# A hybrid encoder step: sums of squares on GpSimd, a root moved into the head, and three reorderings

## The chip, the cores and the metric

The kernel runs on one core of a Trainium2 chip. A core has a matrix engine (TensorE, PE in the profile, with weight loads as PEld), a vector engine (VectorE, DVE), a scalar engine (ScalarE, ACT), GpSimd (POOL) and SyncE (SP), which here only issues DMAs. Each engine works through its own queue in order; semaphores order the engines among each other. SBUF is the memory on the core, PSUM the accumulators that TensorE writes. The metric is the device time of one execution in microseconds (us), lower is better.

## The reference

One layer of a streaming encoder, for 512 new frames of a prompt and 32 of a running stream, D = 2048:

```
xn = rmsnorm(x, g_mix)
z = xn @ w_in                    # conv gates, h, q, k, v and 8 forget logits
x = x + concat(rmsnorm(gated short conv), rmsnorm(forgetting attention)) @ w_out
x = x + cross_attention(rmsnorm(x, g_xattn), 256 memory tokens) @ w_xo
x = x + square(relu(rmsnorm(x, g_mlp) @ w_up)) @ w_down      # hidden 8192
y = rmsnorm(x, g_final)
```

`rmsnorm` divides by the root of the mean square over the 2048 channels of a frame. Beside y, the new keys, values, forget values, conv rows and memory keys and values are returned. All is float32.

## The kernel before

Activations lie with channels on the 128 partitions and the T = 544 frames along the row, so x is 16 tiles of 128x544, read in two column halves of 272. Each float32 operand is split (`split`, L84 and L85) into a high part, rounded by ScalarE to the matrix engine's format, and a low part, the rest, subtracted by VectorE; each product is three matmuls (high-high, high-low, low-high). Most of the large products are done in a seven-product form (Strassen's kind): sums and differences of weight blocks ("sum", L230 and L1261) and of activation blocks ("operands", L199 to L213, whose sums are `ts`) are formed on VectorE.

A norm's sum of squares is kept per frame in two 128x544 accumulators, one for each half of the 16 tiles: ScalarE squares a tile into a buffer `sq`, and a DMA issued by GpSimd adds it to the accumulator in SBUF. `rstd` (L170 on) then sums over partitions by TensorE (`ssq`), and takes the root by ScalarE's Ln and Exp and four VectorE instructions per half. Since g is applied to the rows first, the root r is multiplied in after the product.

The stages, by time: the **head** (0 to 60 us), eight steps j, each with two tiles of x (`xr`), 512 KB of weights, the operands, and 48 matmuls into eight PSUM halves (L362 to L394), which are then copied to the `first_tiles` hr, gc, gb, hr; the forget logits (`emit_logf`, L430, to 70 us); the pairs of in-projection products, conv gating and attention (to 870); memory values and the cross-attention output, called **xo** here (917 to 960), which per tile m adds to the reloaded x (`x2r`), stores it (`x3d`), squares it and applies the gain; the MLP's up products (960 to 1655); the down products (1650 to 2333), whose 8 output pairs p are gone through in four chunks c, with forms of the hidden rows stored to DRAM (`fd`, `bd`) by GpSimd and loaded again; and the **end** (2333 to 2365), four last products of 2x2 kind (L1380 to L1401), the last root (`last_rstd`) and the stores of y.

The order of each engine's queue is set when the kernel is built. A scheduler puts out instructions in the order in which the code emits them, except that it fills idle time with later work that is ready, and that weight splits and roots carry a higher priority. So code that is moved may or may not move instructions. Buffers come from pools of a fixed depth: `tmp` has 7 slots for sq, x2r, h and others; `rstd` has 3, which the forms' `fp` use too; the MLP's `raw2` has 4.

The function `begin` runs between the products of the first pair: it takes the root of x, multiplies the four first tiles by it (L579), hands them to the gating code `kinds`, and evacuates the forget logits (`evac_logf`, z at L435). `forms_in_parts` (L1177 on) gives three steps for each of the last two hidden rows, `differences`, `first` (four `put`s) and `second` (four `put`s), one of which runs after each output pair p of the first chunk.

Of the kernel before, what the change touches and what calls it, by code (L numbers as in the profile page):

```python
# [8 lines left out]
F32 = mybir.dt.float32  # L9
F32R = mybir.dt.float32r  # L10
AF = mybir.ActivationFunctionType
ALU = mybir.AluOpType
# [11 lines left out]
H = 8  # L24
# [17 lines left out]
def hybrid_step(  # L42
# [115 lines left out]

    def accumulate(acc, sq, first):
        if first:  # L160
            dve.tensor_copy(acc, sq)
        else:
            dve.tensor_tensor(acc, acc, sq, ALU.add)
# [35 lines left out]
    def operands(x, b11, ts, tags):  # L199
        hi, lo = two(b11)[:, 0], two(b11)[:, 1]  # L200
        split(hi, lo, x[:, 0])
# [160 lines left out]
    for j in range(8):  # L362
        xr = [headp.tile([128, T], F32, tag="xr", name="xr", bufs=5) for i in range(2)]
        if j == 0:
            hi, lo = weights(w_first[j])
        for i in range(2):
            sp.dma_start(xr[i], xT[j + 8 * i])
        if j:
            hi, lo = weights(w_first[j])
        x = headp.tile([128, 4, TH], F32, tag="x", name="x", bufs=2)  # L370
        for i in range(2):
            if j + i == 0:
                dve.tensor_scalar(x[:, :2], two(xr[i]), gain(G_MIX, 0), None, ALU.mult)
# [14 lines left out]
        for i in range(2):  # L388
            if j:
                sq = tmp("sq")[:, :T]  # L390
                act.activation(sq, xr[i], AF.Square)
                pool.dma_start(acc_x[i], sq, accum_op=ALU.add)
            else:
                act.activation(acc_x[i], xr[i], AF.Square)  # L394
# [13 lines left out]
    for t, ps in ((2, heads[2]), (3, heads[3]), (0, heads[0]), (1, heads[1])):  # L408
        for a in range(2):
            act.activation(two(first_tiles[t])[:, a], ps[a], AF.Copy)  # L410
# [161 lines left out]
    ps = emit_logf()  # L572
    nxt = fetch_pair(0)
    box = {}

    def begin():
        rstd(acc_x, D, out=rb)
        for t, (n, j) in enumerate((("hr", 0), ("gc", 0), ("gb", 0), ("hr", 1))):
            dve.tensor_tensor(first_tiles[t], first_tiles[t], rb, ALU.mult)  # L579
# [513 lines left out]
    def xo_done(m, ps):  # L1093
# [4 lines left out]
        if j == 0:  # L1098
            act.activation(acc_3[i], x, AF.Square)
        else:  # L1100
# [390 lines left out]
```

## Time and profile before

| | us |
|---|---|
| median of 3 runs | 2367.64 (2362.61 to 2367.76) |
| the profiled execution's own time | 2366.75 |
| its span | 2364.9 |
| busy: TensorE, VectorE, ScalarE, GpSimd | 2310.9, 2008.1, 1317.8, 246.8 |
| mean granted TensorE clock | 0.994 |
| accumulating DMAs (acc<-sq) | 40 of 272 KB, 4.9 to landing |
| first product of the head | 8.24 after the span's start |
| last product | ended about 2351; the span ends at 2364.9 |

TensorE is the bound over nearly the whole span. In the page's 40 slices its busy share is below nine tenths only in the first slice, and in slices at the xo stage, the forms and the end. Idle time in brackets in the time lines is the time for which an engine stood before an instruction, and behind the arrow is what ended it.

### The profile page before, as it was taken

How to read it: one execution, taken by the hardware profiler on the slowest of the kernel's cores; microseconds unless marked ns; L12 is line 12 of the kernel's file. 1: busy time of each engine (PE TensorE's matmuls, PEld its weight loads, DVE VectorE, ACT ScalarE, POOL GpSimd, SP SyncE). 2: the span in 40 equal slices, each digit the busy share in tenths (PEclk: the TensorE clock that was granted, in tenths of full speed). 3: DMA queues.
4: the chain of work that ended last, by engine and by line, in shares of the span. 5: the costliest groups of instructions: out<-in, count | busy, mean ns of one | idle time of the engine just before them, and what ended most of it. 6: DMA issues, size and time to landing. Idle time of an engine off the chain costs nothing. (4 is left out here: it accounts for less than half of the span.)

```text
span 2364.9 us, 47573 instructions
## 1 busy us (share of the span) xinstructions
PE 2310.9 (98%) x18083; PEld 2281.7 (96%) x18083; DVE 2008.1 (85%) x3562; ACT 1317.8 (56%) x2569; POOL 246.8 (10%) x447
## 2 busy tenths in 40 slices
PE   8999999999999999899999999999899999999997
PEld 8899999999999998899999999999799999999997
DVE  7899988877767757999999999998788888888885
ACT  8454555555644546665566656665455555555564
POOL 2000011113200001111111111111000000000001
PEclk9999999999999999999999999999999999999998
DMA  9333345578434537655666556668773564565454
GB/s 249 117 105 129 109 159 167 164 233 306 145 93 153 161 104 221 204 192 190 203 191 203 182 188 202 192 196 290 272 252 129 206 240 159 171 234 208 128 174 123
DMA packets 169638, 434.31 MB, mean 184 GB/s; under 512 B 19960, under 2 KB 24752, under 8 KB 169408
## 3 DMA queue, kind: packets, MB, share of 16 engines
q1 hardware_dynamic: 111616, 315.90, 39.8%
q0 software_dynamic: 52288, 106.45, 15.4%
q10 hardware_dynamic: 5504, 8.93, 1.1%
q8 instruction: 141, 2.31, 0.4%
q14 instruction: 89, 0.73, 0.1%
HBM read 322.27 MB, written 97.78 MB: 178 GB/s over the span
## 5 line engine op out<-in xcount | busy, mean ns | idle before, releaser
L84 ACT ACTIVATE whi<-raw 128x512 fp32r<-128x512 f32 x661 | 416.5, 631 | 466.8 <-PE mmx L269 95.4
L84 ACT ACTIVATE whi<-sum 128x512 fp32r<-128x512 f32 x676 | 422.4, 630 | 416.5 <-PE mmx L269 186.2
L85 DVE TENSOR_TENSOR wlo<-raw,whi 128x512 fp32r<-128x512 f32 x661 | 453.4, 688 | 123.5 <-ACT whi L84 115.8
L85 DVE TENSOR_TENSOR wlo<-sum,whi 128x512 fp32r<-128x512 f32 x676 | 453.1, 686 | 88.1 <-ACT whi L84 85.3
L1276 PE MATMUL dx<-f,whi 128*128 128x272 f32 x2016 | 389.6, 289 | 14.3 <-ACT e L1350 7.9
L269 PE MATMUL mmx<-oph,wlo 128*128 128x272 f32 x1296 | 374.9, 289 | 2.6 <-DVE wlo L85 2.6
L269 PE MATMUL mmx<-oph,whi 128*128 128x272 f32 x1296 | 373.5, 288 | 1.3 <-ACT h L278 0.9
L269 PE MATMUL mmx<-opl,whi 128*128 128x272 f32 x1296 | 372.1, 287 | 0.0
L1276 PEld LDWEIGHTS dx<-f,whi 128*128 128x128 f32 x2016 | 317.6, 189 | 16.5 <-ACT e L1350 9.7
L1276 PE MATMUL mm<-f,whi 128*128 128x272 f32 x1512 | 292.1, 288 | 0.0
L1276 PE MATMUL dx<-f,wlo 128*128 128x272 f32 x1008 | 291.3, 289 | 0.0
L269 PE MATMUL mmy<-oph,whi 128*128 128x272 f32 x864 | 249.8, 289 | 6.3 <-ACT whi L84 5.1
L269 PE MATMUL mmy<-oph,wlo 128*128 128x272 f32 x864 | 249.1, 289 | 0.9 <-DVE wlo L85 0.9
L269 PE MATMUL mmy<-opl,whi 128*128 128x272 f32 x864 | 248.8, 288 | 0.0
L269 PEld LDWEIGHTS mmx<-oph,wlo 128*128 128x128 f32 x1296 | 244.0, 188 | 3.2 <-DVE wlo L85 3.2
L269 PEld LDWEIGHTS mmx<-oph,whi 128*128 128x128 f32 x1296 | 244.7, 189 | 1.9 <-ACT h L278 1.1
L269 PEld LDWEIGHTS mmx<-opl,whi 128*128 128x128 f32 x1296 | 244.2, 188 | 0.0
L1276 PEld LDWEIGHTS mm<-f,whi 128*128 128x128 f32 x1512 | 238.2, 189 | 0.0
L1276 PE MATMUL mm<-f,wlo 128*128 128x272 f32 x756 | 218.1, 289 | 0.0
L1276 PEld LDWEIGHTS dx<-f,wlo 128*128 128x128 f32 x1008 | 190.6, 189 | 0.0
L269 PEld LDWEIGHTS mmy<-oph,whi 128*128 128x128 f32 x864 | 162.9, 189 | 7.5 <-ACT whi L84 5.5
L269 PE MATMUL mmx<-b,whi 128*128 128x272 f32 x864 | 167.8, 291 | 1.3 <-DVE x2r L1095 1.1
(412 smaller groups left out, 4941.5 us busy)
## 6 DMA issues: line engine op xcount, KB each, us to landing
raw<-in_w_up SPq DMA_DIRECT2D x128, 512.0 KB, 3.8
raw<-in_w_dn SPq DMA_DIRECT2D x128, 512.0 KB, 4.6
f<-fd SPq DMA_DIRECT2D x224, 272.0 KB, 5.7
fd<-form POOLq DMA_DIRECT2D x180, 272.0 KB, 4.0
raw<-in_w_in SPq DMA_DIRECT2D x88, 512.0 KB, 3.9
raw<-in_w_out SPq DMA_DIRECT2D x32, 512.0 KB, 3.9
acc<-sq POOLq DMA_DIRECT2D x40, 272.0 KB, 4.9
kq<-hl POOLq DMA_DIRECT2D x32, 256.0 KB, 3.1
```

Of the source, the lines that this page charges most:

```text
L84: act.activation(hi, src, AF.Copy)
L85: dve.tensor_tensor(lo, src, hi.bitcast(F32), ALU.subtract)
L269: pe.matmul(ps, a[:, c], x, start=first and j == 0 and n == 0, stop=j == 7 and n == 2, skip_group_check=not first)
L1276: pe.matmul(ps, a[:, c], f[:, x], start=first and j == 0 and n == 0, stop=j == 3 and n == 2, skip_group_check=not first)
```

## The change

Six edits that leave what is computed as it is.

1. The new helper `pool_sum` replaces the accumulating DMA in xo (`acc_3`) and in the last chunk (`acc_4`): ScalarE squares into a `tmp` buffer and GpSimd adds. In the head GpSimd also takes the squares themselves.
2. In the head's first step the loads go xr, half of the weights, xr, the other half; VectorE's first tile and the splits of b12 and b11 stand ahead of the second tile.
3. The eight PSUM halves of the head are copied in the order 0, 2, 3, 1, the first column half by ScalarE and the second by VectorE.
4. The root of x, the four multiplications (now on GpSimd) and `evac_logf` are emitted right behind the forget logits. `begin` keeps the scaled root and the gating.
5. `forms_in_parts` gives nine steps per hidden row, one `put` each; one step is run after each output pair, past the first chunk if need be.
6. At the end, of the first half's outputs two are done by VectorE and three by GpSimd ahead of the last product's addition, the other three by VectorE behind it; a store of y is one piece of 2176 bytes per partition, in a new layout of the output array that the host undoes.

```
@@ -156,6 +156,12 @@
     def gain(off, k):
         return vec[:, off + k:off + k + 1]
 
+    def pool_sum(acc, src, first):
+        sq = acc if first else tmp("sq")[:, :T]
+        act.activation(sq, src, AF.Square)
+        if not first:
+            pool.tensor_tensor(acc, acc, sq, ALU.add)
+
     def accumulate(acc, sq, first):
         if first:
             dve.tensor_copy(acc, sq)
@@ -198,7 +204,6 @@
 
     def operands(x, b11, ts, tags):
         hi, lo = two(b11)[:, 0], two(b11)[:, 1]
-        split(hi, lo, x[:, 0])
         t = ts.rearrange("p (a b c) -> p a b c", a=2, b=2)
         x4 = x.rearrange("p (a b) c -> p a b c", a=2)
         o = {"b11": (hi, lo)}
@@ -361,21 +366,35 @@
     xops = []
     for j in range(8):
         xr = [headp.tile([128, T], F32, tag="xr", name="xr", bufs=5) for i in range(2)]
+        if j:
+            for i in range(2):
+                sp.dma_start(xr[i], xT[j + 8 * i])
+            hi, lo = weights(w_first[j])
+        else:
+            raws = [wpool.tile([128, 1024], F32, tag="raw", name="raw", bufs=3)[:, :512] for i in range(2)]
+            for i in range(2):
+                sp.dma_start(xr[i], xT[8 * i])
+                sp.dma_start(raws[i], w_first[0, :, 512 * i:512 * i + 512])
+            hi, lo = halves(raws[0], 512)
+        x = headp.tile([128, 4, TH], F32, tag="x", name="x", bufs=2)
         if j == 0:
-            hi, lo = weights(w_first[j])
+            dve.tensor_scalar(x[:, :2], two(xr[0]), gain(G_MIX, 0), None, ALU.mult)
+        else:
+            for i in range(2):
+                act.activation(x[:, 2 * i:2 * i + 2], two(xr[i]), AF.Identity, scale=gain(G_MIX, j + 8 * i))
         for i in range(2):
-            sp.dma_start(xr[i], xT[j + 8 * i])
-        if j:
-            hi, lo = weights(w_first[j])
-        x = headp.tile([128, 4, TH], F32, tag="x", name="x", bufs=2)
-        for i in range(2):
-            if j + i == 0:
-                dve.tensor_scalar(x[:, :2], two(xr[i]), gain(G_MIX, 0), None, ALU.mult)
-            else:
-                act.activation(x[:, 2 * i:2 * i + 2], two(xr[i]), AF.Identity, scale=gain(G_MIX, j + 8 * i))
+            sq = tmp("sq")[:, :T] if j else acc_x[i]
+            pool.tensor_tensor(sq, xr[i], xr[i], ALU.mult)
+            if j:
+                pool.tensor_tensor(acc_x[i], acc_x[i], sq, ALU.add)
         b12 = two(headp.tile([128, T], F32R, tag="b12", name="b12", bufs=2))
         split(b12[:, 0], b12[:, 1], x[:, 1])
         b11 = formp.tile([128, T], F32R, tag="b11", name="b11")
+        split(two(b11)[:, 0], two(b11)[:, 1], x[:, 0])
+        if j == 0:
+            act.activation(x[:, 2:], two(xr[1]), AF.Identity, scale=gain(G_MIX, 8))
+            more = halves(raws[1], 512)
+            hi, lo = Parts([hi, more[0]]), Parts([lo, more[1]])
         o = operands(x, b11, headp.tile([128, 2 * T], F32, tag="ts", name="ts"), "ABC")
         xops.append(o)
         for i, xs in enumerate(((o["b11"], (b12[:, 0], b12[:, 1])), (o["b21"], o["b22"]))):
@@ -385,13 +404,6 @@
                     for a in range(2):
                         pe.matmul(ps[a], w[:, c], xs[a][q], start=j + i == 0 and n == 0,
                                   stop=j + i == 8 and n == 2)
-        for i in range(2):
-            if j:
-                sq = tmp("sq")[:, :T]
-                act.activation(sq, xr[i], AF.Square)
-                pool.dma_start(acc_x[i], sq, accum_op=ALU.add)
-            else:
-                act.activation(acc_x[i], xr[i], AF.Square)
     wf_hl = tpool.tile([128, T + 4], F32R, tag="t", name="wf_hl")[:, :256].rearrange("p (k c) -> p k c", k=KD)
     split(wf_hl[:, :, 0:8], wf_hl[:, :, 8:16], wf)
     head_cm.__exit__(None, None, None)
@@ -405,9 +417,9 @@
         return keepp.tile([128, T + 4], F32, tag="keep", name=name)
 
     first_tiles = [tmp("hr0")[:, :T], tmp("gc0")[:, :T], tmp("gb0")[:, :T], kept("hr1")[:, :T]]
-    for t, ps in ((2, heads[2]), (3, heads[3]), (0, heads[0]), (1, heads[1])):
-        for a in range(2):
-            act.activation(two(first_tiles[t])[:, a], ps[a], AF.Copy)
+    for t in (0, 2, 3, 1):
+        act.activation(two(first_tiles[t])[:, 0], heads[t][0], AF.Copy)
+        dve.tensor_copy(two(first_tiles[t])[:, 1], heads[t][1])
 
     rb = npool.tile([128, T], F32, tag="rstd", name="rb", bufs=3)
     rbs = npool.tile([128, T], F32, tag="rstd", name="rbs", bufs=3)
@@ -570,16 +582,16 @@
 
     steps = (lambda: gate_open(box["z"]), gate_exp, gate_log, gate_close, gate_sum, turn_logf)
     ps = emit_logf()
+    rstd(acc_x, D, out=rb)
+    for t in range(4):
+        pool.tensor_tensor(first_tiles[t], first_tiles[t], rb, ALU.mult)
+    box = {"z": evac_logf(ps)}
     nxt = fetch_pair(0)
-    box = {}
 
     def begin():
-        rstd(acc_x, D, out=rb)
+        dve.tensor_scalar(rbs, rb, SCALE, None, ALU.mult)
         for t, (n, j) in enumerate((("hr", 0), ("gc", 0), ("gb", 0), ("hr", 1))):
-            dve.tensor_tensor(first_tiles[t], first_tiles[t], rb, ALU.mult)
             kinds[n][1](j, first_tiles[t])
-        box["z"] = evac_logf(ps)
-        dve.tensor_scalar(rbs, rb, SCALE, None, ALU.mult)
 
     def job(i):
         (n1, j1), (n2, j2) = pairs[i]
@@ -1095,17 +1107,13 @@
         dve.tensor_tensor(two(x), two(x), ps[:, :, :TH], ALU.add)
         sp.dma_start(x3d[m], x)
         j, i = m % 8, m // 8
-        if j == 0:
-            act.activation(acc_3[i], x, AF.Square)
-        else:
-            sq = (tmp("sq") if j > 4 else up.tile([128, 1024], F32, tag="raw2", name="sq", bufs=4))[:, :T]
-            act.activation(sq, x, AF.Square)
-            pool.dma_start(acc_3[i], sq, accum_op=ALU.add)
+        pool_sum(acc_3[i], x, j == 0)
         if i == 0:
             xgs[j] = up.tile([128, 2 * T], F32, tag="sum", name="x").rearrange("p (a b) -> p a b", a=4)
         act.activation(xgs[j][:, 2 * i:2 * i + 2], two(x), AF.Identity, scale=gain(G_MLP, m))
         if i:
             b11 = upform.tile([128, T], F32R, tag="b11", name="b11")
+            split(two(b11)[:, 0], two(b11)[:, 1], xgs[j][:, 0])
             ops.append(operands(xgs.pop(j), b11, up.tile([128, 2 * T], F32, tag="sum", name="ts"), "ABC"))
 
     def fetch_up(i, last=True):
@@ -1191,18 +1199,13 @@
             dve.tensor_tensor(t12[:, 1], b[:, 1], t12[:, 0], ALU.subtract)
             dve.tensor_tensor(t34[:, 1], b[:, 0], t12[:, 1], ALU.subtract)
 
-        def first():
-            put(fd[i][0], a[:, 0])
-            put(bd[i - NF + 4], a[:, 1])
-            put(fd[i][5], b[:, 0])
-            put(fd[i][3], b[:, 1])
-
-        def second():
-            for t, q in zip(box["t"], ((1, 2), (4, 6))):
-                for n in range(2):
-                    put(fd[i][q[n]], t[:, n])
-
-        return [differences, first, second]
+        steps = [differences]
+        for dst, x in ((fd[i][0], a[:, 0]), (bd[i - NF + 4], a[:, 1]), (fd[i][5], b[:, 0]), (fd[i][3], b[:, 1])):
+            steps.append(lambda dst=dst, x=x: put(dst, x))
+        for n, q in enumerate(((1, 2), (4, 6))):
+            for k in range(2):
+                steps.append(lambda n=n, k=k, q=q: put(fd[i][q[k]], box["t"][n][:, k]))
+        return steps
 
     rb_3 = []
 
@@ -1309,20 +1312,14 @@
         return r
 
     def store(p, a, y):
-        d = slice(TH * a, TH * a + TH)
-        (sp if p % 2 else act).dma_start(o_y[2 * p:2 * p + 2, :, d].rearrange("m p t -> p m t"), two(y))
+        (sp if p % 2 else act).dma_start(o_y[a, p], y)
 
     def complete(p):
         for a in range(2):
             fin[a, p] = slot("AB"[a], F32, "yout")
         for i in range(2):
             m = 2 * p + i
-            if p == 0:
-                act.activation(acc_4[i], x3[m], AF.Square)
-            else:
-                sq = tmp("sq")[:, :T]
-                act.activation(sq, x3[m], AF.Square)
-                pool.dma_start(acc_4[i], sq, accum_op=ALU.add)
+            pool_sum(acc_4[i], x3[m], p == 0)
             for a in range(2):
                 act.activation(two(fin[a, p])[:, i], two(x3[m])[:, a], AF.Identity, scale=gain(G_FIN, m))
 
@@ -1366,8 +1363,8 @@
             dve.tensor_tensor(xb[:, 0], xb[:, 0], X, ALU.add)
             if c + 1 < NF // 4 and p < 7:
                 nf[p] = load_form(c + 1, p)
-            if c == 0 and 1 <= p <= len(parts):
-                parts[p - 1]()
+            if parts and c + p:
+                parts.pop(0)()
             if c == NF // 4 - 1:
                 complete(p)
         if c < NF // 4 - 1:
@@ -1377,6 +1374,12 @@
     ws = [[doperand(a11), doperand(a12)], [doperand(a21), doperand(a22)]]
     hs = ((fs[0], fs[5]), (b12, fs[3]))
     sums = []
+
+    def pooled(r):
+        rp = tmp("rb")[:, :TH]
+        act.activation(rp, r, AF.Copy)
+        return rp
+
     for a in range(2):
         y = fin[a, 7] = slot("AB"[a], F32, "yout")
         sums.append([t[:, TH * a:TH * a + TH] for t in acc_4])
@@ -1394,14 +1397,17 @@
             act.activation(sq, xa, AF.Square)
             sums[a].append(sq)
             act.activation(two(y)[:, i], xa, AF.Identity, scale=gain(G_FIN, 14 + i))
-            if a:
-                if i == 0:
-                    rb_4 = last_rstd(sums[0])
-                for p in range(4 * i, 4 * i + 4):
+            if a and i == 0:
+                rb_4 = last_rstd(sums[0])
+                rb_5 = pooled(rb_4)
+                for p in (0, 1):
                     store(p, 0, finish((0, p), rb_4, dve))
+                for p in (2, 3, 4):
+                    store(p, 0, finish((0, p), rb_5, pool))
+    for p in (5, 6, 7):
+        store(p, 0, finish((0, p), rb_4, dve))
     rb_4 = last_rstd(sums[1])
-    rb_5 = tmp("rb")[:, :TH]
-    act.activation(rb_5, rb_4, AF.Copy)
+    rb_5 = pooled(rb_4)
     for p in range(8):
         store(p, 1, finish((1, p), rb_5 if p in (2, 4, 7) else rb_4, pool if p in (2, 4, 7) else dve))
     down_cm.__exit__(None, None, None)
...
```

What the order of the instructions shows at three places. **GpSimd in the head**: before, the 14 accumulating DMAs stand in one block behind the constants:

```order
L146 MEMSET mask_p 128x128
L194 MEMSET sel_111 16x8
L147 AFFINE_SELECT mask_p<-mask_p 128x128
L196 AFFINE_SELECT sel_111<-sel_111 16x8 x2
L392 DMA acc<-sq 128x544 x14
L535 DMA yd_0_902<-ych 128x544
```

and after the change, from the second tile on and at the end of the block:

```order
L387 TENSOR_TENSOR acc<-xr 128x544
L202 AFFINE_SELECT sel_111<-sel_111 16x8
L387 TENSOR_TENSOR sq<-xr 128x544 x2
L389 TENSOR_TENSOR acc<-acc,sq 128x544 x2
L387 TENSOR_TENSOR sq<-xr 128x544
L389 TENSOR_TENSOR acc<-acc,sq 128x544
...
L389 TENSOR_TENSOR acc<-acc,sq 128x544
L587 TENSOR_TENSOR hr_887<-hr_887,rb 128x544
L587 TENSOR_TENSOR gc_888<-gc_888,rb 128x544
L587 TENSOR_TENSOR gb_889<-gb_889,rb 128x544
L587 TENSOR_TENSOR hr_890<-hr_890,rb 128x544
L547 DMA yd_0_904<-ych 128x544
```

The squares and sums of each tile now stand one behind the other on GpSimd, 30 in all before the first multiplication by `rb`, and the four multiplications of L579 follow them here as L587.

**ScalarE at the last forms** (`fp` are the forms' high parts, e the products' copies, `whi` weights; acc and h their source). Before:

```order
L1350 ACTIVATE e_22755<-dx 128x272
L84 ACTIVATE whi<-raw 128x512
L1352 ACTIVATE e_22756<-mm 128x272
L84 ACTIVATE whi<-raw_22749 128x512
L1355 ACTIVATE e_22755<-dx 128x272
L84 ACTIVATE fp<-acc 128x272
L84 ACTIVATE whi<-raw 128x512
L84 ACTIVATE fp<-acc 128x272
L84 ACTIVATE whi<-sum 128x512
L1360 ACTIVATE e_22756<-dx 128x272
```

After:

```order
L1347 ACTIVATE e_22731<-dx 128x272
L84 ACTIVATE whi<-raw 128x512
L1349 ACTIVATE e_22732<-mm 128x272
L84 ACTIVATE whi<-raw_22725 128x512
L1352 ACTIVATE e_22731<-dx 128x272
L84 ACTIVATE whi<-raw 128x512
L84 ACTIVATE fp<-acc 128x272
L84 ACTIVATE whi<-sum 128x512
L1357 ACTIVATE e_22732<-dx 128x272
L84 ACTIVATE fp<-acc 128x272
```

One `fp` went behind a split of weights. The other rows of the 16 `fp` stand in the same places as before.

**SyncE at xo**, where `raw` and `raw_1...` are MLP weights. Before:

```order
L1084 DMA x2r<-x2d_7080 128x544
L1084 DMA x2r<-x2d_7088 128x544
L1084 DMA x2r<-x2d_7081 128x544
L220 DMA raw<-in_w_up 128x1024
L1096 DMA x3d_11778<-x2r 128x544
L1096 DMA x3d_11786<-x2r 128x544
L1084 DMA x2r<-x2d_7089 128x544
L1084 DMA x2r<-x2d_7082 128x544
```

After:

```order
L1096 DMA x2r<-x2d_7081 128x544
L1096 DMA x2r<-x2d_7089 128x544
L1096 DMA x2r<-x2d_7082 128x544
L225 DMA raw<-in_w_up 128x1024
L225 DMA raw_12836<-in_w_up 128x1024
L225 DMA raw_12838<-in_w_up 128x1024
L225 DMA raw_13136<-in_w_up 128x1024
L1108 DMA x3d_11780<-x2r 128x544
L1108 DMA x3d_11788<-x2r 128x544
L225 DMA raw_13138<-in_w_up 128x1024
L1108 DMA x3d_11781<-x2r 128x544
L1096 DMA x2r<-x2d_7090 128x544
```

Two loads of x2r fewer and three loads of MLP weights more stand ahead of the first store of x3d.

More of the change, by code (lines that the diff above doesn't have):

```diff
@@ L1461 @@
     outs = {
-        "y": (KD, 128, T), "k": (H, 128, T), "v": (H, 128, T), "logf": (H, T), "conv": (128, 8, 4),
+        "y": (2, 8, 128, T), "k": (H, 128, T), "v": (H, 128, T), "logf": (H, T), "conv": (128, 8, 4),
         "mk": (HX, 128, NMEM), "mv": (NMEM, 512),
@@ L1471 @@
     o = {k: np.asarray(r.results[0][f"out_{k}"]) for k in outs}
-    yT = o["y"].reshape(D, T).T
+    yT = o["y"].reshape(2, 8, 128, 2, TH).transpose(0, 4, 1, 3, 2).reshape(T, D)
     kv = {n: o[n].transpose(2, 0, 1) for n in ("k", "v")}
```

## The prediction

> **What bounds the kernel now.** I read the page's busy times first, then the table of windows over the stages that the diff touches, then the time line of single engines inside those stages, and last the waits and the landing times of transfers.
>
> ```profile
> PE 2310.9 (98%) x18083; PEld 2281.7 (96%) x18083; DVE 2008.1 (85%) x3562; ACT 1317.8 (56%) x2569; POOL 246.8 (10%) x447
> ```
>
> TensorE is busy for 2310.9 us of a span of 2364.9, and the change removes no product. What it can win lies in the roughly 54 us in which TensorE stands or in stretches with a low granted clock, and only in the parts of them that the diff touches. The columns of the next table are the stretch, its length, then busy time and (count) of each engine, the granted clock, the share of DMA time and GB/s.
>
> ```profile
> 10.00:50.00 40.00, 40.00 (x305) 40.00 (x305) 37.48 (x78) 39.29 (x75) 10.53 (x12) 1.00 0.98 260
> 50.00:60.00 10.00, 9.46 (x76) 9.23 (x74) 4.13 (x8) 4.59 (x12) 1.72 (x2) 1.00 0.87 199
> 60.00:75.00 15.00, 14.48 (x118) 12.25 (x119) 6.79 (x8) 3.46 (x8) 0.00 (x0) 1.00 0.43 163
> 90.00:95.00 5.00, 2.72 (x14) 2.51 (x14) 5.00 (x11) 1.93 (x3) 0.40 (x1) 0.78 0.00 0
> 95.00:105.00 10.00, 9.07 (x66) 8.66 (x65) 10.00 (x23) 3.45 (x7) 0.71 (x2) 0.94 0.37 109
> 950.00:1000.00 50.00, 43.30 (x314) 41.70 (x313) 44.54 (x78) 31.89 (x59) 6.97 (x10) 0.93 0.62 191
> 2270.00:2340.00 70.00, 69.15 (x544) 68.05 (x543) 52.97 (x91) 50.04 (x107) 10.35 (x12) 1.00 0.45 109
> ```
>
> In the head (10 to 50) TensorE never stands, but ScalarE has 39.29 of 40 us and VectorE 37.48: three engines are full together, and VectorE has 2.5 us to spare. That matters below. At 90 to 105, and at 950 to 1000, VectorE or ScalarE is late and TensorE waits.
>
> **The change part by part, 1: the start.** The time line of the start, us from the span's start, with idle time and its releaser in brackets:
>
> ```profile
> 5.66 1.29 DVE L85 TENSOR_TENSOR wlo<-raw,whi 128x512 fp32r<-128x512 f32 x2 [5.66 <-ACT whi L84]
> 6.05 0.64 ACT L394 ACTIVATE acc<-xr 128x544 f32<-128x544 f32 x1
> 6.87 0.50 DVE L373 TENSOR_SCALAR x<-xr,vec 128x544 f32<-128x544 f32 x1
> 7.46 0.73 ACT L84 ACTIVATE b<-x 128x272 fp32r<-128x272 f32 x2
> 8.24 1.64 PE L386 MATMUL mm<-b,whi 128*128 128x272 f32 x5 [8.24 <-ACT b L84]
> ```
>
> The first product waits for b, which waits for x on VectorE, which stood behind two splits of weights. After the change x's rows are loaded first, x is VectorE's first work, and no square stands on ScalarE ahead of b. The square and one of the two weight splits leave the chain: 0.64 + 1.29/2 = 1.3 us. The earlier landing of xr comes on top: VectorE's first row then is x and no longer a weight split at 5.66, and the first weight split on ScalarE waits for half as many bytes. No row prices that; I take 2.0 in all, with 1 and 3 as ends, and not more, because the second half of the weights lands as late as before and may be missing at once.
>
> **2: the end of the head.** `hr`, `gc` and `gb` are copied out of PSUM by ScalarE alone; TensorE waits for a bank:
>
> ```profile
> 60.52 2.15 PE L430 MATMUL mm<-b,wf_hl 128*16 128x272 f32 x16 [1.06 <-ACT hr L410]
> 62.11 1.22 DVE L230 TENSOR_TENSOR sum<-raw,raw 128x1024 f32<-128x1024 f32 x1 [7.53 <-DMA raw<-in_w_in]
> ```
>
> VectorE is idle for 7.53 us there, and takes half of the eight copies, the bank that is wanted first first. I take 1.0 (0.5 to 1.1).
>
> **3: the root moved into the head.** Now VectorE does the root and the four multiplications while TensorE is already in the first pair:
>
> ```profile
> 82.39 0.43 DVE L181 TENSOR_TENSOR nt<-rb 128x272 f32<-128x272 f32 x1
> 85.28 0.44 DVE L184 TENSOR_TENSOR rb<-rb,nt 128x272 f32<-128x272 f32 x1
> 86.24 0.72 DVE L579 TENSOR_TENSOR hr<-hr,rb 128x544 f32<-128x544 f32 x1
> 88.85 0.72 DVE L579 TENSOR_TENSOR hr<-hr,rb 128x544 f32<-128x544 f32 x1
> 92.88 0.60 PE L269 MATMUL mmx<-oph,wlo 128*128 128x272 f32 x1 [2.28 <-DVE wlo L85]
> 101.59 0.39 PE L269 MATMUL mmx<-oph,whi 128*128 128x272 f32 x1 [0.93 <-ACT h L278]
> 95.44 0.70 DVE L435 TENSOR_TENSOR z<-mm,rb 16x544 f32<-16x544 f32 x1
> ```
>
> VectorE is without a gap from 90 to 105. What leaves that stretch: the root, 82.39 to 85.72 less two small copies, about 3; four multiplications at a spacing of 0.64, 2.6 (to GpSimd); z, 0.6. That is over 6 us against 2.28 + 0.93 = 3.2 us of standing and a clock of 0.78 and 0.94, which costs 0.22 x 2.72 + 0.06 x 9.07 = 1.1 more. The root goes where VectorE has 6.79 of 15 us. GpSimd's four multiplications are needed only by the gating of the first pair, some 15 us later; at its price (part 5) they take 5.2. If that cover failed, the first pair's VectorE work would wait, not TensorE at first. I take 4.0 of the 4.3 (2 to 4.3).
>
> **4: the step into the MLP.** 14 accumulating DMAs stop. ScalarE, TensorE, and the landing time of the accumulating DMA whose `sq` held the slot:
>
> ```profile
> 960.15 0.66 ACT L1102 ACTIVATE sq<-x2r 128x544 f32<-128x544 f32 x1 [3.36 <-issue]
> 951.94 0.88 POOL L1103 DMA_DIRECT2D acc<-sq  x1 [3.14 <-DMA acc<-sq]
> acc<-sq POOLq DMA_DIRECT2D x1, 272.0 KB, 8.1
> 964.12 0.59 PE L269 MATMUL mmy<-oph,whi 128*128 128x272 f32 x1 [3.10 <-ACT whi L84]
> 966.05 0.82 PE L269 MATMUL mmx<-b,whi 128*128 128x272 f32 x2 [1.12 <-DVE x2r L1095]
> 978.53 0.39 PE L269 MATMUL mmy<-oph,whi 128*128 128x272 f32 x1 [1.96 <-ACT whi L84]
> ```
>
> The DMA issued at 951.94 took 8.1 us, so its slot came free at 960.04, and the next square starts at 960.15: ScalarE's 3.36 us are the DMA's. TensorE then stands 3.10 + 1.12 + 1.96, and 0.39 in a smaller wait, 6.6, and the clock of 0.93 costs 0.07 x 43.3 = 3. In the changed order nearly all squares take a slot that a GpSimd sum frees, and the weights of the MLP are asked for before the stores of x3d, not behind them (they no longer wait for the slots that squares held). Against it: only five, not seven, loads of x2r stand ahead of those weights, so a later x2r can be late, and two stores per pair still hold slots. I take 6.0 of 9.6, with 2 and 9 as ends.
>
> **5: sums of squares on GpSimd.** The nearest row of such work, and the rows of the ScalarE squares that go in the head:
>
> ```profile
> L1293 POOL TENSOR_TENSOR yout<-yout,rb 128x544 f32<-128x544 f32 x3 | 3.9, 1325 | 18.0 <-ACT rb L1404 18.0
> L1293 DVE TENSOR_TENSOR yout<-yout,r 128x544 f32<-128x544 f32 x13 | 8.5, 715 | 0.5 <-ACT rb L1404 0.5
> L391 ACT ACTIVATE sq<-xr 128x544 f32<-128x544 f32 x14 | 8.3, 644 | 0.0
> ```
>
> Three in 3.92 us: 1.31 each. In the head 16 multiplications and 14 additions, 30 x 1.31 = 39 us; four per step of 6 us, 5.2, so GpSimd keeps up and frees the xr slots in time, if it runs undisturbed. The price on the path is then 0, the cover being TensorE's 6 us per step; ScalarE is 16 x 0.64 = 10 us lighter, which buys nothing while TensorE is full. In the last chunk 12 additions, 15.7 us, lie in 70. The one row with both engines adding shows VectorE at 715 ns beside GpSimd's 1325, but there VectorE reads r from PSUM. No row shows GpSimd reading while VectorE reads two operands from SBUF, as nearly all its work in the head does. That price lies between 0 and 39 us in the head. I take 0, from the nearest row, and keep the rest as a rival.
>
> The Trainium skill, "SBUF — State Buffer", "Who interferes with whom", speaks against me: a VectorE instruction with two SBUF inputs contends with a GpSimd instruction that reads SBUF, over a shared port pair that is locked for a whole instruction. By that rule the sum would come out near the first rival's 2385, by the nearest row at 2352; no run here shows the pairing yet.
>
> **6: forms one at a time.** ScalarE's `fp` waits for an earlier form's store, and TensorE behind it:
>
> ```profile
> 1660.78 0.43 ACT L84 ACTIVATE fp<-acc 128x272 fp32r<-128x272 f32 x1 [5.95 <-DMA fd<-fp]
> 1684.28 0.43 ACT L84 ACTIVATE fp<-h 128x272 fp32r<-128x272 f32 x1 [5.97 <-DMA fd<-fp]
> 1727.44 0.43 ACT L84 ACTIVATE fp<-acc 128x272 fp32r<-128x272 f32 x1 [3.10 <-DMA fd<-fp]
> ACT fp L84 <- DMA fd<-fp: 19.4, 7, 6.0
> ```
>
> 19.4 us of waits in 7 places is the largest loss in reach. But the code that spreads the steps does not spread the instructions: ScalarE's rows there stand as before, apart from the last `fp`, which goes behind a split of weights. I take 1.0, at most the 3.10 of that last wait, at least 0.
>
> **7: the end.** VectorE's rows:
>
> ```profile
> 2346.57 2.62 DVE L1293 TENSOR_TENSOR yout<-yout,r 128x544 f32<-128x544 f32 x4
> 2349.10 0.43 DVE L1392 TENSOR_TENSOR x<-x,mm 128x272 f32<-128x272 f32 x1
> 2349.45 2.61 DVE L1293 TENSOR_TENSOR yout<-yout,r 128x544 f32<-128x544 f32 x4
> 2351.98 0.43 DVE L1303 TENSOR_SCALAR v<-ssq 128x272 f32<-128x272 f32 x1
> ```
>
> The last x stands behind four outputs, and the last v behind four more. With two and three, each block is shorter by 1.3 and 0.65 us; v then waits for ScalarE's exponential, not for outputs. GpSimd's three have 6 us before the second half. I take 1.5 (0.5 to 2.5; whole rows of y in one piece may help the last stores).
>
> **The sum.** 2.0 + 1.0 + 4.0 + 6.0 + 0 + 1.0 + 1.5 = 15.5 us off the profiled execution's 2366.75 (span 2364.9 and 1.85 around it): 2351.2. The median is 0.9 above that execution: **2352**. The ends of the terms add up to 6 and 23, so this case's own range is 2345 to 2362.
>
> **Rivals.** *One port for two engines* (slower). Each GpSimd instruction then holds VectorE off for its 1.31 us. In the head VectorE has 2.5 us idle from 10 to 50 and 5.9 from 50 to 60; 39 - 8.4 = 31 us remain, and since VectorE was within 2.5 us of TensorE's pace, nearly all of it lands on the path. In the step into the MLP, 14 x 1.31 = 18 us over some 50 us meet 5.5 us of idle VectorE (950 to 1000), but TensorE's pace there leaves ScalarE room, so I count 3 of the gain there as gone. The last chunk has 17 us of room for 15.7. 31 + 3 - 15.5 gives +18: about 2385. Half of it, if only some instructions collide, is even. It decides from 15 us on, which is 12 of the 30 instructions. For it: VectorE's fullness in the head; against it: only that no measured row shows it. The Trainium skill's rule ("SBUF — State Buffer") would make this case true.
>
> *The MLP's step keeps its stall.* x2r or x3d takes the place of the DMA that went, at 8 us landing, and the head's start brings nothing since data come no faster (98% DMA share): 15.5 - 6 - 2 = 7.5, or less if weights ahead of x2r cost 3 to 6: 2360 to 2366.
>
> *The forms do spread*, because ScalarE's waits move with the DMAs even in an unchanged order: of TensorE's stretch at 1655 to 1730 another 10 to 15 us come back: 2338.
>
> **Chances.** Forecast 0.46, shared port 0.36, stall kept 0.13, forms 0.05. About 0.3% (7 us) is what a measurement of this kernel tells from no change, so faster means under 2360.5 and slower over 2374.7. Faster: nearly all of the forecast (0.44), the forms (0.05), a third of the stall case (0.04), a weak collision (0.03): 0.56. Slower: most of the shared port, 0.31. The rest, 0.13, within. Both signs are likely, so the range reaches from the middle of the forecast's lower half, 2343, to the shared port's 2385.
>
> **What would show it.** Per step: the first product near 6.2; no wait of 1 us ahead of the logf products; no standing at 90 to 102; ScalarE's square without 3 us at the xo step; `fp` waits still near 19; last v behind the exponential. Wrong first of all if VectorE's splits in the head take longer than 0.69 us for 512 columns or wait with no releaser named, and TensorE's products there are spaced wider; then the windows from 10 to 50 show TensorE below 40 and the logf products start after 70 and not near 59.

## The result: 30.5 us slower

The changed kernel takes 2398.07 us (median of 4 runs, 2397.06 to 2399.81) where the kernel before takes 2367.55: a ratio of 1.0135, 95% interval 1.0117 to 1.0152. The forecast was 2352. The busy times of the page after:

```profile
PE 2319.7 (97%) x18083; PEld 2285.8 (95%) x18083; DVE 2055.0 (86%) x3559; ACT 1310.4 (55%) x2550; POOL 322.2 (13%) x470
```

VectorE has 47 us more busy time with three instructions fewer, and ScalarE 7 us less. The table gives the length of each stage in the two profiled executions, from the start of its first product to that of the next stage's; the row of xo's products ends at the start of the last one with high parts of weights, so TensorE's wait ahead of the MLP counts as MLP up. The spans are 2364.9 and 2398.0, and the last column adds up to the 33.1 between them. The down products have eight chunks, not the four that the description of the kernel before gives; a quarter is about two of them.

| stage | before | after | difference |
|---|---|---|---|
| span's start to the first product | 8.24 | 6.49 | -1.7 |
| head, to the first logf product | 52.27 | 77.20 | +24.9 |
| logits, pairs, attention, to the first w_out product | 484.63 | 484.39 | -0.2 |
| to the products of xo's last eight tiles, whose weights are split on the way | 391.63 | 392.14 | +0.5 |
| those products | 23.71 | 29.65 | +5.9 |
| MLP up | 688.81 | 690.47 | +1.7 |
| first quarter of the down products, with the late forms | 184.87 | 184.20 | -0.7 |
| the other three quarters | 498.78 | 500.42 | +1.6 |
| the four last products, to the start of the last one's last matmul | 13.89 | 13.89 | 0.0 |
| from there to the end | 18.12 | 19.21 | +1.1 |

Between executions whose code is the same in a stage, MLP up and the first quarter of down differ by up to 4 us, so their rows show nothing by themselves; xo and the last three quarters agree within 0.2 us. Counted up to the MLP's first product, xo takes 27.3 and 32.7 us, so 5.4 more.

The head first. The windows of after, with the columns of the prediction's table:

```profile
10.00:50.00 40.00, 24.54 (x160) 23.88 (x161) 39.57 (x43) 16.10 (x31) 32.82 (x21) 0.87 0.39 131
50.00:60.00 10.00, 6.13 (x46) 5.69 (x45) 10.00 (x13) 5.00 (x10) 5.14 (x4) 0.98 0.21 70
```

From 10 to 50 us VectorE is busy 39.57 of 40 us (37.48 before), but with 43 instructions where 78 were. Its time lines and GpSimd's show what it is busy with. GpSimd, then VectorE:

```profile
3.74 1.09 POOL L387 TENSOR_TENSOR acc<-xr 128x544 f32<-128x544 f32 x1 [1.94 <-DMA xr<-in_xT]
...
7.72 2.13 POOL L387 TENSOR_TENSOR sq<-xr 128x544 f32<-128x544 f32 x2
9.82 2.60 POOL L389 TENSOR_TENSOR acc<-acc,sq 128x544 f32<-128x544 f32 x2
12.39 1.08 POOL L387 TENSOR_TENSOR sq<-xr 128x544 f32<-128x544 f32 x1
...
62.67 14.10 POOL L387 TENSOR_TENSOR sq<-xr 128x544 f32<-128x544 f32 x1 [7.37 <-DMA xr<-in_xT]
```

```profile
5.63 0.44 DVE L85 TENSOR_TENSOR b<-x,b 128x272 fp32r<-128x272 f32 x1 [0.50 <-ACT b L84]
...
7.62 6.15 DVE L85 TENSOR_TENSOR b<-x,b 128x272 fp32r<-128x272 f32 x1
13.70 1.85 DVE L210 TENSOR_TENSOR ts<-x 128x544 f32<-128x544 f32 x1
15.48 1.61 DVE L85 TENSOR_TENSOR opl<-x,oph 128x544 fp32r<-128x544 f32 x1
...
62.90 0.43 DVE L85 TENSOR_TENSOR b<-x,b 128x272 fp32r<-128x272 f32 x1
63.25 0.71 DVE L210 TENSOR_TENSOR ts<-x 128x544 f32<-128x544 f32 x1
...
75.98 3.17 DVE L85 TENSOR_TENSOR opl<-ts,oph 128x544 fp32r<-128x544 f32 x2 [0.17 <-ACT oph L84]
```

A subtraction that took 0.44 us takes 6.15: GpSimd runs five instructions one behind the other from 7.72 to 13.5, and VectorE's ends just behind them. Then the two take turns, so that `ts` needs 1.85 in place of 0.71. At 62.67 it is the other way: one multiplication that takes 1.09 alone takes 14.10, while VectorE goes on at its old durations, without a gap until it stands for 0.17 us at 75.8; the multiplication ends 1 us later, at 76.77. Another one, of 4.89 us from 36.19 on, ends 1 us after VectorE's next idle time too. So a run of instructions without a gap can keep the other engine out. It does not always: from 13.7 us on both have work in a row and take turns, and what decides between the two cases is not shown. TensorE waits for VectorE:

```profile
13.83 0.82 PE L405 MATMUL mm<-b,whi 128*128 128x272 f32 x2 [6.29 <-DVE b L85]
...
32.45 0.82 PE L405 MATMUL mm<-b,whi 128*128 128x272 f32 x2 [7.90 <-DVE b L85]
...
83.69 2.14 PE L442 MATMUL mm<-b,wf_hl 128*16 128x272 f32 x16
```

From its first product to the logf products TensorE is busy 55.4 us, where it was 51.2 before. So of the 24.9 us that the head lost, 20.7 are standing. The other 4.2 are the same products taking longer, at a granted clock of 0.87 from 10 to 50 us and 0.94 from 60 on, where it was 1.00 before.

At the end, TensorE and ScalarE:

```profile
2383.99 1.20 PE L1302 MATMUL ssq<-sq,inv 128*128 128x272 f32 x2 [3.49 <-ACT sq L1397]
```

```profile
2380.54 2.92 ACTq L1315 DMA_DIRECT2D out_y<-yout  x3
2383.51 0.43 ACT L1397 ACTIVATE sq<-x 128x272 f32<-128x272 f32 x1 [4.42 <-POOL yout L1296]
```

The last square waits for GpSimd's outputs, of which it uses none (why, below at *The end*).

### The profile page after: what moved, and what is told of

Same layout as the page of the kernel before. It is cut to its first block, busy times and chain, and to the rows that moved or that the text cites. A ratio compares the mean times of both kernels' runs of the same rounds, so it can differ in the third digit from the quotient of the medians.

```text
span 2398.0 us, 47547 instructions
## 1 busy us (share of the span) xinstructions
PE 2319.7 (97%) x18083; PEld 2285.8 (95%) x18083; DVE 2055.0 (86%) x3559; ACT 1310.4 (55%) x2550; POOL 322.2 (13%) x470
## 5 line engine op out<-in xcount | busy, mean ns | idle before, releaser
L85 DVE TENSOR_TENSOR wlo<-raw,whi 128x512 fp32r<-128x512 f32 x661 | 460.3, 699 | 116.4 <-ACT whi L84 108.7
L85 DVE TENSOR_TENSOR wlo<-sum,whi 128x512 fp32r<-128x512 f32 x676 | 459.3, 695 | 82.5 <-ACT whi L84 80.3
```

The costliest lines, as they stand in the source:

```text
L85: dve.tensor_tensor(lo, src, hi.bitcast(F32), ALU.subtract)
```

## The experiments

Theory: GpSimd instructions that read SBUF and VectorE instructions with two operands in SBUF keep each other out, and that is nearly all of the loss. Rivals: the new load order or late xr buffers stretch the head; the slots of the squares stretch xo; the root or the single forms cost something.

**The head's sums undone.** head_dma is the changed kernel with ScalarE's squares and the accumulating DMA in the head:

```
-            sq = tmp("sq")[:, :T] if j else acc_x[i]
-            pool.tensor_tensor(sq, xr[i], xr[i], ALU.mult)
-            if j:
-                pool.tensor_tensor(acc_x[i], acc_x[i], sq, ALU.add)
...
+                act.activation(sq, xr[i], AF.Square)
+                pool.dma_start(acc_x[i], sq, accum_op=ALU.add)
```

> The changed kernel with one part undone: in the head ScalarE squares and the accumulating DMA adds, as before; load order, copies, root behind the logits, xo, last chunk and end stay changed. Theory (GpSimd's reads hold VectorE off): the head loses its 24.9 us, the logf products start near 58 to 60 us instead of 83.7, and the total is 2371 to 2378. Rival (the new load order or late xr buffers stretch the head, not the port): the logf products still start after 75 and the total stays above 2388.

2370.80 us: ratio 1.0014 (1.0004 to 1.0024) to before, 27.3 under the changed kernel. Its logf products start at 57.1. The load order and the copies are innocent: with them the head, from the first product to the logf products, is 51.0 where before had 52.3.

**The port by itself.** Three kernels based on before leave out the head's squares and sums behind the first two tiles, so their outputs are not the reference's. lock_none does only that; lock_tt and lock_memset also give GpSimd work that no part of the kernel waits for:

```
+    idle = headp.tile([128, T], F32, tag="idle", name="idle")
+    pool.memset(idle, 0.0)
     for j in range(8):
+        for i in range(4):
+            pool.tensor_tensor(idle, idle, idle, ALU.mult)     # lock_tt; in lock_memset: two pool.memset(idle, 0.0)
```

> The kernel before without any sums of squares in the head beyond its first two tiles (14 squares and 14 accumulating DMAs left out, so the root is of two tiles alone). A control for the next two. Both theories: within 2 us of the kernel before, since TensorE is full in the head anyway: 2363 to 2369.

> The control plus 32 multiplications of an idle 128x544 tile by itself on GpSimd, that nothing waits for and that wait for nothing (same part of the sums left out). Theory (port): 32 x 1.31 = 42 us of GpSimd beside a full VectorE, 20 to 34 us more than the control, VectorE's 512-column splits in the head at 1.3 us and more instead of 0.69. Rival (late data or buffers): as the control, within 2 us, since no data of the kernel passes GpSimd.

> The control plus 64 memsets of the same idle tile on GpSimd, which write and read nothing (same part of the sums left out). Theory (only reads of SBUF contend with VectorE's second operand): as the control, within 2 us, splits at 0.69 us. A wider theory (any GpSimd instruction in SBUF holds VectorE off): 15 us or more above the control.

lock_none: 2368.92, ratio 1.0005 (0.9994 to 1.0015). lock_tt: 2395.37, ratio 1.0118 (1.0097 to 1.0138). lock_memset: 2370.50, ratio 1.0013 (1.0003 to 1.0024). The groups of VectorE from 10 to 50 us, and of GpSimd (count, then busy us and mean ns), in lock_none, where GpSimd has no such work:

```profile
L85 DVE TENSOR_TENSOR wlo<-raw,whi 128x512 fp32r<-128x512 f32 x14 | 9.5, 682 | 0.0
L85 DVE TENSOR_TENSOR b<-x,b 128x272 fp32r<-128x272 f32 x14 | 5.9, 432 | 0.0
L153 DVE COPY mask_s<-mask_p 32x32 f32<-32x32 f32 x4 | 0.7, 173 | 0.1
```

in lock_tt:

```profile
L85 DVE TENSOR_TENSOR b<-x,b 128x272 fp32r<-128x272 f32 x7 | 8.1, 1197 | 0.0
L85 DVE TENSOR_TENSOR wlo<-raw,whi 128x512 fp32r<-128x512 f32 x5 | 6.9, 1397 | 0.0
L153 DVE COPY mask_s<-mask_p 32x32 f32<-32x32 f32 x4 | 2.4, 598 | 0.0
...
L366 POOL TENSOR_TENSOR idle<-idle 128x544 f32<-128x544 f32 x32 | 41.1, 1285 | 2.4
```

and in lock_memset:

```profile
L85 DVE TENSOR_TENSOR b<-x,b 128x272 fp32r<-128x272 f32 x14 | 5.9, 433 | 0.0
L85 DVE TENSOR_TENSOR wlo<-raw,whi 128x512 fp32r<-128x512 f32 x13 | 8.8, 684 | 0.0
L153 DVE COPY mask_s<-mask_p 32x32 f32<-32x32 f32 x4 | 2.3, 585 | 0.0
...
L366 POOL MEMSET idle<- 128x544 f32 x32 | 17.9, 560 | 1.8
L367 POOL MEMSET idle<- 128x544 f32 x32 | 17.7, 552 | 1.8
```

41 us of multiplications that have no data in common with the kernel cost 26.5 us; 36 us of memsets cost 1.6. Splits take 1397 ns beside the first and 684, as in lock_none, beside the second. So GpSimd's work that reads SBUF collides with them, and work that only writes it does not. The head of lock_memset is still 3.9 us longer than lock_none's (55.5 to 51.6), and its rows say why: the eight small copies, about 170 ns each in before, take 603 and 585 on average. The Trainium skill, "SBUF — State Buffer", "Who interferes with whom", says both: two-input instructions contend with GpSimd's reads alone, copies can go through both of VectorE's ports and then contend with GpSimd too. The first the runs show; the second they show as a delay, by 0.4 us for each of eight copies.

**All of GpSimd's arithmetic beside VectorE undone.** no_gp has, beside head_dma's edit, before's accumulating DMAs in xo and the last chunk, and the four multiplications by the root on VectorE. xo_only and xo_slots are before with GpSimd's addition in xo alone, the first with the squares in tmp slots as in the change, the second with before's buffers:

```
-            pool.dma_start(acc_3[i], sq, accum_op=ALU.add)
+            pool.tensor_tensor(acc_3[i], acc_3[i], sq, ALU.add)     # xo_slots
```

> The changed kernel with all GpSimd arithmetic beside VectorE undone: accumulating DMAs again in the head, in xo (with the buffers of before) and in the last chunk, and the four multiplications by the root on VectorE, behind the logits. Load order, copies, root in the head, forms one at a time and the end stay changed. Theory (the port is the only loss): head 3.4 us ahead of before as without GpSimd there, the first pairs 2 to 4 ahead, xo and the last chunk as before, so 2359 to 2363, slower only at the end by 1 to 2. Rival (the root in the head and the single forms cost something themselves): 2366 and more, with the time lost before 550 us or between 1650 and 1830.

> The kernel before with the edit of xo alone: the squares of x2r in tmp slots, added by GpSimd. Theory (port): the last xo product ends 4 to 7 us later than in before, 960.5. With the buffers a part of it.

> The kernel before with GpSimd's addition in xo in the place of the accumulating DMA, but with the buffers for the squares and the order of loads as before. Theory (port alone): as late at the last xo product as the run with the whole edit, 4 to 7 us. Rival (five and not seven loads of x2r ahead, and squares in the slots of x2r): within 1 us of before here, and the loss only in the run with the whole edit.

no_gp: 2361.29, ratio 0.9976 (0.9965 to 0.9986): what is left of the change is faster than before by 5.9 us. xo takes 23.7 there, as in before, and 29.6 in xo_only and 29.8 in xo_slots (2373.88 and 2374.80, one run each). The buffers and the load order make no difference; GpSimd's 14 additions do. The stage also tests which VectorE work is hit. In one of its groups one operand lies in PSUM (`x2r<-x2r,mm`), in another both lie in SBUF (`ts<-x`); from 920 to 985 us in before, then in xo_slots:

```profile
L1095 DVE TENSOR_TENSOR x2r<-x2r,mm 128x544 f32<-128x544 f32 x14 | 10.0, 715 | 0.4 <-PE mm L120 0.4
L205 DVE TENSOR_TENSOR ts<-x 128x544 f32<-128x544 f32 x8 | 5.8, 724 | 8.1 <-ACT x L1106 8.1
```

```profile
L1095 DVE TENSOR_TENSOR x2r<-x2r,mm 128x544 f32<-128x544 f32 x14 | 9.9, 710 | 0.0
L205 DVE TENSOR_TENSOR ts<-x 128x544 f32<-128x544 f32 x8 | 9.1, 1141 | 4.9 <-ACT x L1106 4.9
```

Of these two only the second got longer, as did most of the other groups with both operands in SBUF (the splits of `raw` from 685 to 1068 ns; `opl<-x` did not). Few of the first overlap an addition there; at the end of no_gp, ten outputs with the root in PSUM run beside GpSimd's and keep 0.71 us each.

TensorE's waits in xo (for what, us in all, times, longest), of no_gp and of xo_slots:

```profile
PE mmy L274 <- ACT whi L84: 5.8, 2, 3.8
PE mmx L274 <- DVE x2r L1109: 1.1, 1, 1.1
```

```profile
PE mm L120 <- DVE x2r L1095: 5.3, 7, 1.7
PE mmy L269 <- ACT whi L84: 4.2, 2, 2.5
```

In before and no_gp TensorE stands only behind the last products of xo, mostly on ScalarE. With GpSimd's additions VectorE is late seven times more, 5.3 us, and the old stall stays beside it. In the changed kernel, too, TensorE stands 5.1 us among xo's products and then 6.6 us (4.2 + 1.4 + 0.6 + 0.4), as long as in before. In the place of ScalarE's one stand of 3.36 us ahead of a square there are five of at most 1.7, 4.5 us in all, whose releaser the profile does not name. Ahead of the MLP's first product ScalarE now stands for VectorE:

```profile
992.23 0.63 ACT L84 ACTIVATE whi<-sum 128x512 fp32r<-128x512 f32 x1 [3.07 <-DVE sum L235]
```

**The end.** end_fix is no_gp with the copy of the root for GpSimd (`rp`) from another pool, since I took the wait for one on a tmp slot. end_sp is no_gp with the first half's stores issued by SyncE:

```
-        (sp if p % 2 else act).dma_start(o_y[a, p], y)
+        (sp if p % 2 or a == 0 else act).dma_start(o_y[a, p], y)     # end_sp
```

> The run before this one, with one more edit: the ScalarE copy of the root for GpSimd is taken from the pool of roots and not from the seven tmp slots. In the changed kernel the last square waited until GpSimd's three outputs had released such a slot. Theory: that wait (4.4 us idle before the square, some 3 of them on the path) goes, the span between the last product and the end falls from 19.2 to 15 to 17 us (18.1 before the change), and the total is 2 to 3.5 us under the run without this edit. Rival (the wait is for GpSimd as an engine or the stores end last anyway): within 1 us.

> The run without GpSimd arithmetic beside VectorE, with the stores of the first half's outputs all issued by SyncE and none by ScalarE. There the ScalarE queue held a store of GpSimd's third output ahead of the last square, which began 4.5 us after its engine went idle. Theory: the square starts within 1 us of the last addition of x, the last statistic 2 to 3 us earlier, and from the last product to the end it takes 16 to 17 us where it took 19.3; total 2358 to 2360. Rival (the last outputs and stores bound the end): no gain, 19 us.

end_fix: 2361.89, ratio 0.9975 (0.9966 to 0.9985), the wait unchanged at 4.49 us: my reading was wrong. The cause stands in ScalarE's own queue: it issues the stores of even p, and the store of GpSimd's last output waits there ahead of the square. ScalarE in no_gp, then in end_sp:

```profile
2341.69 2.93 ACTq L1322 DMA_DIRECT2D out_y<-yout  x3
2344.72 0.43 ACT L1409 ACTIVATE sq<-x 128x272 f32<-128x272 f32 x1 [4.49 <-POOL yout L1303]
```

```profile
2341.19 0.43 ACT L1409 ACTIVATE sq<-x 128x272 f32<-128x272 f32 x1 [1.76 <-DVE x L1407]
```

end_sp: 2358.65, ratio 0.9963 (0.9954 to 0.9972); from the last product to the end 16.55 us, where no_gp has 19.33 and before 18.12.

**The forms.** fp_tmp is end_sp with the forms' buffers from the tmp slots, which e1 and e2 of each output pair go through as well; fp_three is that with the three steps of before:

```
-            f = npool.tile([128, T], F32R, tag="rstd", name="fp", bufs=3)
+            f = tpool.tile([128, T + 4], F32R, tag="t", name="fp")[:, :T]
```

> The run before this one, and the forms' buffers fp taken from the seven tmp slots that the output pairs' e1 and e2 also go through, in the place of three slots of their own. In the order of the instructions one fp now stands in each output pair, which nine single steps alone did not do. Theory (the forms' stall comes from three slots that wait for stores while ScalarE is filled with fp): the waits of fp on stores go from 19 us to under 3, TensorE from the first product of the MLP's second half to a quarter of it is 12 to 16 us shorter, total 2343 to 2348. Rival (the stall is elsewhere in the start of that stage, the loads of x3d and forms at 7 us landing): less than 5 us gained.

> The same with the three steps of before in the place of nine single ones, so four forms stand in each of four output pairs. Theory: the slots make most of the gain, the nine steps the rest: 2 to 8 us more than the run with single steps. If single steps are worth nothing even with the slots: within 2 us of it.

fp_tmp: 2344.33, ratio 0.9900 (0.9885 to 0.9914), the fastest of all, 23.8 us under before. fp_three: 2348.00 (one run). ScalarE's waits of fp from 1640 to 1860 us, in end_sp, in fp_three, and what is left in fp_tmp:

```profile
ACT fp L84 <- DMA fd<-fp: 19.8, 8, 6.1
ACT fp L84 <- DMA bd<-fp: 1.3, 1, 1.3
```

```profile
ACT fp L84 <- DMA fd<-fp: 3.2, 2, 3.0
ACT fp L84 <- DMA bd<-fp: 1.8, 1, 1.8
```

```profile
ACT whi L84 <- ACT fp L84: 0.5, 2, 0.3
```

The first quarter of the down products takes 180.7, 173.4 and 167.9. The stall came from the three slots: with a slot free, the scheduler filled ScalarE with the next fp, however the steps were cut, and the queue then stood until a store landed. On the tmp slots the three steps of before already gain 7.2 of the 12.8 us. With nine steps one fp then falls to each output pair, 10.5 us apart, and that brings the other 5.6, in one profiled execution each. On the three slots, nine steps (180.7 to 184.2 us in five kernels) and three (182.4 to 186.5 in eight) cannot be told apart. No run gives the forms seven slots of their own, so how much comes from more slots and how much from slots shared with the output pairs is open.

**Additions on VectorE in xo.** xo_dve is fp_tmp with the last six of xo's accumulating DMAs (j over 4) as VectorE additions:

```
+            if j > 4:
+                dve.tensor_tensor(acc_3[i], acc_3[i], sq, ALU.add)
+            else:
                 pool.dma_start(acc_3[i], sq, accum_op=ALU.add)
```

> The run with forms through tmp slots, and in xo the last six sums of squares added by VectorE (0.7 us each) where an accumulating DMA held the slot of a square. Theory: ScalarE's 3.4 us wait before the last squares goes, VectorE has room for 4.3 us of additions in the last 18 us, and the first products of the MLP come 2 to 5 us earlier. Rival (VectorE is the bound of that stretch, or the wait for weights of the MLP takes the stall's place): within 2 us either way.

2345.59, ratio 0.9904 (0.9888 to 0.9921), no gain over fp_tmp. fp_tmp's ScalarE stands 5.77 us before the third last square; that wait is gone, and TensorE waits for VectorE in its place:

```profile
PE mm L120 <- DVE x2r L1109: 3.4, 2, 3.2
```

**The root.** root_only is before with the root, the four multiplications and z behind the logits, on VectorE; root_gp has the multiplications on GpSimd:

```
     ps = emit_logf()
+    rstd(acc_x, D, out=rb)
+    for t in range(4):
+        dve.tensor_tensor(first_tiles[t], first_tiles[t], rb, ALU.mult)     # pool in root_gp
+    box = {"z": evac_logf(ps)}
```

> The kernel before with the root of x, the four multiplications and the logits' evacuation emitted behind the logits, all on VectorE; nothing else changed. Theory (the stall moves: VectorE stays without a gap from 70 to 100 us and the second pair's gating stands ahead of the sums of weights): the way from the last logf product to the mixer's output product gets shorter by 0 to 1.5 us only. The prediction's step: 4 us shorter.

> The same with the four multiplications on GpSimd. Theory (port): four instructions of 1.3 us hold VectorE off in a stretch where it has no gap, so 2 to 5 us of VectorE time are lost, and the same way is 0.5 to 3 us longer than with VectorE doing them. If the port cost nothing there: 1 us shorter, since VectorE is relieved of 2.6 us.

2362.52 and 2365.05, one run each (before beside them 2367.37). The way from the last logf product to the first w_out product is 474.9 in before (up to 475.3 in other kernels with its code there), 472.4 in root_only, 472.9 in root_gp. In no_gp, end_fix, end_sp, fp_tmp, fp_three and xo_dve, whose code there is the same, it is 474.3, 472.8, 474.2, 472.7, 472.7 and 472.8; in the changed kernel 474.7. So the root moved ahead brings 0.6 to 2.5 us on VectorE, less than the 4 of the prediction. GpSimd's four in root_gp, and a VectorE row beside them:

```profile
77.81 2.35 POOL L575 TENSOR_TENSOR gb<-gb,rb 128x544 f32<-128x544 f32 x1
```

```profile
78.86 3.61 DVE L85 TENSOR_TENSOR wlo<-sum,whi 128x512 fp32r<-128x512 f32 x2
```

Two splits take 3.61 in place of 1.28, so the relief of 2.6 us goes at least in part in the collision. What that costs on the way is not shown: root_gp's 0.5 us over root_only is less than what kernels with the same code differ by. In no_gp VectorE is busy 12.97 of 13 us from 72 to 85, and TensorE's waits are smaller, not gone:

```profile
95.98 0.39 PE L274 MATMUL mmy<-oph,wlo 128*128 128x272 f32 x1 [0.87 <-DVE wlo L85]
```

Why the same code falls on either of two values 1.5 us apart is open.

## Why the prediction was wrong

The failed step is part 5, "I take 0, from the nearest row". The nearest row had VectorE read one operand from PSUM, and the two groups of xo_slots show that this made it no witness. The price lay nearer the other end of the bounds: of 39 us, the head lost 24.9 against before and 26.2 (77.2 to 51.0) against the same loads and copies without GpSimd's sums. The first rival had the mechanism, the place and nearly the price: it put 31 us in the head and 3 in xo; they were 26 and 5.9, and 1.6 in the last chunk, where I had called the 17 us of idle time enough (in no_gp, with the DMAs back, these 1.6 us are gone). It came out at 2385 and not 2398 because it kept the forecast's 15.5 us of gains, of which 3 came. By the Trainium skill's rule ("SBUF — State Buffer", "Who interferes with whom") it should have been the forecast. The rival's picture of one wait for each GpSimd instruction was too simple, though: single waits went up to 6.15 us one way and 14.10 the other.

The other parts, in order:

1. The start: 2.0 predicted, 1.7 measured (2.1 in head_dma). Right.
2. The end of the head: 1.0 predicted; 1.3 in head_dma's head, where no wait stands ahead of the logf products. Right, though the heads of kernels with before's code differ by 1 us themselves.
3. The root: 4.0 predicted, 0.2 measured in the change, 0.6 to 2.5 with VectorE alone. The mechanism held only in part. The count of VectorE time that leaves was right, but GpSimd's four multiplications took 8.1 us in root_gp and not 5.2 and held VectorE up, and VectorE stays full from 72 us on, so that a part of the wait comes back a few us later.
4. The step into the MLP: a gain of 6.0 predicted, a loss of 5.9 in xo measured. The stall that I priced is real, and the one long wait for the DMA's slot went. But TensorE's 6.6 us stay whole, since VectorE takes the DMA's place, and the lateness of VectorE in xo comes on top. With the additions on VectorE (xo_dve) VectorE is late as well. The rival *The MLP's step keeps its stall* was right that the stall stays; the waits that have a name are for VectorE and not for x2r or x3d, as it had assumed, and what held ScalarE's five short ones is open.
6. The forms: 1.0 predicted, 0.7 measured, within the scatter. The reading of the order was right: cutting the steps does not spread them. The third rival's size of what can come back, 10 to 15 us, was right as well: 12.8 us in fp_tmp against end_sp, by another edit.
7. The end: 1.5 gained predicted, 1.1 lost measured. I looked at VectorE's queue and not at the store that stood in ScalarE's. With the store elsewhere the gain is 1.6.

## What to carry to other kernels

A second elementwise engine is no free engine: ask of each instruction where its operands lie, and take a row as a price only if both engines read from the same memories as in the planned work. A DMA issue is an instruction of the queue that issues it, so whoever stores the output of a slow engine waits for it. Cutting the forms into steps did not pace them, since the scheduler fills idle time; the buffers that they share with the loop did.

## What the runs showed of the hardware

- Where both read two operands from SBUF, GpSimd and VectorE did not always take turns: a run of instructions held the other engine out for up to 6.15 us (a VectorE subtraction of 0.44) and 14.10 us (a GpSimd multiplication of 1.09), and GpSimd's long waits ended 1 us after VectorE's next idle time of 0.17 and 0.27 us.
- VectorE's instructions with one operand in PSUM kept their 0.71 us beside GpSimd's multiplications.
- GpSimd's memsets, 36 us of them, left VectorE's 512-column splits at 684 ns, but took eight 32x32 copies from 0.17 to 0.6 us.
- With VectorE held off, GpSimd's multiplication of a 128x544 tile by itself takes 1.09 us and its addition of two tiles 1.30.
